# Low parts of the projections' weights: a negated copy by ScalarE and an adding DMA in place of a subtraction on VectorE

## The chip, the cores and the metric

The kernel runs on one core of a Trainium2 chip. The metric is the device time of one execution in microseconds, here the median of 3 runs: 1387.85 us (1387.84 to 1392.62). The profile is of one further execution, which took 1385.42 us; its span, from the first to the last instruction, is 1383.6 us. All times below are of that execution and count from the span's start.

The core has five engines with a program of their own: TensorE (matmuls, PE in the rows; PEld is its weight load), VectorE (DVE), ScalarE (ACT), GpSimd (POOL) and SyncE (SP), which issues most DMAs. DMAs run on 16 shared engines, whoever issues them. Each engine works its instructions off in order and waits on semaphores for others.

## The reference

One decoder block over a sequence of 1024 tokens of width 1024, in float32:

```python
ada = silu(c) @ w_ada + b_ada; sh1, sc1, gt1, sh2, sc2, gt2 = split(ada, 6)
h = rmsnorm(x, norm1_g) * (1 + sc1) + sh1
q, k, v, glu, gates = split(h @ w_in)
a = diff_attention(q, k, v, lam, rel_bias)          # 4 heads, two softmaxes each, causal
a = (rmsnorm(a, attn_sub_g) * (1 - lam_init)) @ w_o_attn
u = causal_depthwise_conv(u_lin * sigmoid(u_gate))  # 31 taps
cv = silu(layernorm(u)) @ w_o_conv + b_o_conv
y = sigmoid(g_attn) * a + sigmoid(g_conv) * cv
x = x + gt1 * (y @ w_out)
h2 = rmsnorm(x, norm2_g) * (1 + sc2) + sh2
fg, fu = split(h2 @ w_ffn_in)
x = x + gt2 * ((silu(fg) * fu) @ w_ffn_out)
return rmsnorm(x, final_g)
```

## The kernel before

Activations lie transposed, channels on the 128 partitions and tokens along the free axis, so a tile is 128 x 1024 and a matmul covers 128 x 512. To keep float32 accuracy with matmuls on a shorter format (fp32r), each operand is split into a high part, the value rounded to fp32r, and a low part, the value minus the high part. A product is then three matmuls, in this order (`mm3`, L203): high weights by high activations, high weights by low activations or the other way round, and one with the low weights. In the projections TensorE issues the one with the low weights third.

The class `Weights` (L171) makes the two parts of a slab of weights of 128 x 1024, in three steps. `load` (L176) fetches the raw weights by a DMA of SyncE (tile `wr_...`). `high` (L185) rounds them on ScalarE (`wh_...`). `low` (L189) subtracts on VectorE (`wl_...`). The pool has two buffers for each of the three tiles, so a part for one slab can be begun when the slab before last is no longer used: for the high and low parts, when its last matmul has ended.

Two planners call these steps ahead of use. In the attention stretch `project` (L679) works through 15 projections in 16 steps of three matmuls each, interleaved by the table `PLAN` with the work of the four heads; in step 2 of a projection it loads the raw weights of the next, in step 5 it makes the high part and in step 9 the low part (`WL`, L60). The first projection has no one before it: its three steps are called at once (L819). Behind the attention, `run` (L1025) goes through a list of jobs: gates of the attention (`ga`), its output projection (`oa`), gates of the convolution (`gc`), its output projection (`oc`), 48 matmuls each, and the common output projection (`wo`), 16 jobs of 24 matmuls. At a job's start it loads the next job's weights and makes their high part; the low part is made behind the first half of the job, in `wo` at its start. Weights of `oa` and `oc` come as two pieces of 512 columns, so their source has three dimensions.

The order of instructions on an engine is set by a scheduler that looks at what is ready, except where `in_order` keeps the order in which the code was written: TensorE in the attention stretch, TensorE and VectorE in the jobs up to `oc`. ScalarE's and GpSimd's orders are the scheduler's up to the FFN. In the convolution's norm (`ConvNorm`, L908), which lies between the jobs of `gc`, ScalarE computes squares, logarithms and exponentials. In `wo`, ScalarE squares each finished piece of x1 for the next norm (`sq`), and GpSimd issues the DMA that stores it (`x1_d`, L1136).

Of the kernel before, what the change touches and what calls it, by code (L numbers as in the profile page):

```python
# [10 lines left out]
F32 = mybir.dt.float32  # L11
F32R = mybir.dt.float32r
AF = mybir.ActivationFunctionType
ALU = mybir.AluOpType
# [85 lines left out]
def tile_hybrid_block(ctx: ExitStack, tc: tile.TileContext, xT, vecs, cvec, lamv, relb, bsel, bmask, jrev,  # L100
# [27 lines left out]
    V, A, T, G = Engine(nc.vector), Engine(nc.scalar), Engine(nc.tensor), nc.gpsimd  # L128
# [42 lines left out]
    class Weights:  # L171
# [15 lines left out]
            split_hi(self.hi[:, :self.n], self.raw[:, :self.n])  # L187

        def low(self):  # L189
            self.lo = wp.tile([P, D], F32R, tag="wlo", name=f"wl_{self.name}")  # L190
            V.tensor_tensor(out=self.lo[:, :self.n], in0=self.raw[:, :self.n], in1=self.hi.bitcast(F32)[:, :self.n],
                            op=ALU.subtract)

        def all(self):
            self.load()
# [698 lines left out]
    with tc.tile_pool(name="ps2", bufs=6, space=bass.MemoryType.PSUM) as ps2, ExitStack() as fxs:  # L894
# [71 lines left out]
        def ga(m, w, low):  # L966
            y.append(xslot(f"y{m}"))
            for hf in range(2):
                ps = (bankG if m == NGA else bank)("ga")
                gemm_half(ps, w, hacts, hf)  # L970
                A.activation(y[m][:, hf_sl(hf)], ps, AF.Sigmoid)
                advance(convs, CG[hf])
                if hf == 0:
                    low()
                    if m == NGA:
                        split_a(range(AS, H))

        def oa(m0, w, low):
            for i, m in enumerate((m0, m0 + 1)):
                for hf in range(2):  # L980
                    ps = bank("oa")
                    gemm_half(ps, [t[:, i * HB:(i + 1) * HB] for t in w], aacts, hf)
                    V.tensor_tensor(out=y[m][:, hf_sl(hf)], in0=ps, in1=y[m][:, hf_sl(hf)], op=ALU.mult)
                    advance(convs, CO[i])
                    if i == 0 and hf == 1:
                        low()
# [164 lines left out]
        class Pair:  # L1151
# [4 lines left out]
            n = HB  # L1156
# [111 lines left out]
        class Group(Pair):  # L1268

            n = GP * P  # L1270
# [269 lines left out]
        n = len(grp)  # L1540
# [132 lines left out]
```

## Time and profile before

| | |
|---|---|
| median of the runs | 1387.85 us |
| profiled execution, its span | 1385.42 us, 1383.6 us |
| TensorE busy | 1333.2 us (96%) |
| VectorE busy | 1067.0 us (77%) |
| ScalarE busy | 636.8 us (46%) |
| GpSimd busy | 104.1 us (8%) |
| attention stretch | about 100 to 363 us |
| `ga` and `oa` | 363 to 483 us |
| `gc` | 483 to 573 us |
| `oc` | 573 to 618 us |
| `wo` | 618 to 709 us |
| FFN and end | from 709 us |

A share of busy time is a mean over stretches with different limits; what a change in one stretch is worth is read in that stretch, from the wait that ends last there. A busy TensorE is not TensorE at its peak, since the ends of matmuls are modelled and overlap: in the stretches above one of 512 columns is begun each 0.23 us, while its row says 0.39.

### The profile page before, as it was taken

How to read it: one execution, taken by the hardware profiler on the slowest of the kernel's cores; microseconds unless marked ns; L12 is line 12 of the kernel's file. 1: busy time of each engine (PE TensorE's matmuls, PEld its weight loads, DVE VectorE, ACT ScalarE, POOL GpSimd, SP SyncE). 2: the span in 40 equal slices, each digit the busy share in tenths (PEclk: the TensorE clock that was granted, in tenths of full speed). 3: DMA queues.
4: the chain of work that ended last, by engine and by line, in shares of the span. 5: the costliest groups of instructions: out<-in, count | busy, mean ns of one | idle time of the engine just before them, and what ended most of it. 6: DMA issues, size and time to landing. Idle time of an engine off the chain costs nothing.

```text
span 1383.6 us, 16481 instructions
## 1 busy us (share of the span) xinstructions
PE 1333.2 (96%) x6070; PEld 1091.0 (79%) x6070; DVE 1067.0 (77%) x1698; ACT 636.8 (46%) x1079; POOL 104.1 (8%) x181
## 2 busy tenths in 40 slices
PE   7999999999999999999997999999999997999996
PEld 5678887877788887788775888888888886888886
DVE  6847698899989897787788677777777765777765
ACT  5546666666511114632575444444444441222355
POOL 0000000000000000000000011111100031212004
PEclk9999999999999999999999999999999999999998
DMA  8511010101112112329621255554444499578203
GB/s 304 192 32 31 32 46 16 47 16 31 46 46 61 46 61 92 137 92 343 234 77 77 76 183 183 182 166 167 157 165 147 150 315 398 203 250 304 74 31 122
DMA packets 58899, 184.43 MB, mean 133 GB/s; under 512 B 6425, under 2 KB 11457, under 8 KB 58818
## 3 DMA queue, kind: packets, MB, share of 16 engines
q1 hardware_dynamic: 38242, 110.49, 24.2%
q0 software_dynamic: 20000, 72.36, 14.7%
q8 instruction: 48, 0.79, 0.2%
q10 hardware_dynamic: 576, 0.52, 0.1%
q14 instruction: 33, 0.27, 0.1%
HBM read 139.83 MB, written 43.52 MB: 133 GB/s over the span
## 4 chain that ended last, share of the span: by engine, by line
PE 68%; issue 11%; DVE 9%; ACT 6%; DMA 5%; POOL 1%; SPq 0%; DVEq 0%; ACTq 0%; POOLq 0%
PE fx L113 19%; PE fz L113 9%; PE proj L113 8%; PE ga L113 5%; PE fy L113 5%; PE gc L113 4%; PE oa L113 3%; PE oc L125 3%; DMA ada<-in_w_ada 3%; PE wo L125 3%; PE sc L113 2%; PE vacc L125 2%; PE av L113 2%; DMA gb<-gs_d 1%; DMA xs<-in_xT 1%
## 5 line engine op out<-in xcount | busy, mean ns | idle before, releaser
L113 ACT ACTIVATE wbp<-tt 128x512 fp32r<-128x512 f32 (+1 forms) x75 | 43.9, 586 | 157.5 <-DVE tt L113 144.2
L113 DVE SCALAR_TENSOR_TENSOR cacc<-u,vec,cacc 128x1022 f32<-128x1022 f32 (+28 forms) x87 | 110.2, 1267 | 2.2
L113 PE MATMUL proj<-hhi,wh_in 128*128 128x512 f32 x239 | 98.3, 411 | 1.7 <-DVE kl L125 1.7
L113 PE MATMUL proj<-hhi,wl_in 128*128 128x512 f32 x240 | 94.0, 392 | 0.0
L113 PE MATMUL proj<-hlo,wh_in 128*128 128x512 f32 x240 | 93.7, 390 | 0.0
L113 ACT ACTIVATE wb<-tt 128x512 fp32r<-128x512 f32 (+1 forms) x59 | 35.4, 602 | 94.6 <-DVE tt L113 87.8
L113 PE MATMUL fx<-A,wb 128*128 128x512 f32 x299 | 70.9, 391 | 2.8 <-DVE g L113 2.8
L113 PE MATMUL fx<-gb,wbp 128*128 128x512 f32 x282 | 68.6, 389 | 0.1
L113 PE MATMUL fx<-S,wbp 128*128 128x512 f32 x276 | 67.1, 391 | 1.4 <-DVE S L113 1.3
L113 PEld LDWEIGHTS fx<-A,wb 128*128 128x128 f32 x299 | 56.0, 188 | 15.3 <-issue 3.7
L113 PE MATMUL fz<-S,wbp 128*128 128x512 f32 x276 | 66.5, 390 | 1.5 <-ACT S L113 1.3
L113 PE MATMUL fz<-S,wb 128*128 128x512 f32 x252 | 61.0, 390 | 1.6 <-DVE S L113 1.6
L113 PEld LDWEIGHTS fx<-S,wbp 128*128 128x128 f32 x276 | 51.6, 188 | 13.5 <-DVE S L113 2.5
L113 PE MATMUL fx<-S,wb 128*128 128x512 f32 x252 | 60.8, 390 | 1.4 <-DVE S L113 1.3
L113 PEld LDWEIGHTS fx<-gb,wbp 128*128 128x128 f32 x282 | 52.8, 188 | 11.5 <-DMA gb<-gs_d 0.5
L113 PEld LDWEIGHTS fz<-S,wbp 128*128 128x128 f32 x276 | 51.7, 188 | 12.9 <-ACT S L113 1.7
L113 DVE SCALAR_TENSOR_TENSOR x1r<-fx,cols,x1r 128x512 f32<-128x512 f32 x48 | 36.0, 751 | 30.6 <-PE fx L113 20.8
L125 ACT ACTIVATE e<-sc,mn 128x512 f32<-128x512 f32 (+7 forms) x64 | 47.2, 740 | 26.8 <-DVE mn L125 25.8
L113 PEld LDWEIGHTS fz<-S,wb 128*128 128x128 f32 x252 | 47.1, 188 | 12.1 <-DVE S L113 2.4
L113 PEld LDWEIGHTS fx<-S,wb 128*128 128x128 f32 x252 | 47.2, 188 | 11.9 <-DVE S L113 1.6
L113 DVE TENSOR_TENSOR wbp<-tt,wbp 128x512 fp32r<-128x512 f32 (+1 forms) x75 | 47.1, 629 | 11.7 <-ACT wbp L113 11.6
L113 PEld LDWEIGHTS proj<-hhi,wh_in 128*128 128x128 f32 x239 | 45.0, 188 | 11.1 <-issue 3.6
(350 smaller groups left out, 3601.9 us busy)
## 6 DMA issues: line engine op xcount, KB each, us to landing
gb<-gs_d POOLq DMA_DIRECT2D x59, 512.0 KB, 10.3
gs_d<-gstw POOLq DMA_DIRECT2D x36, 512.0 KB, 3.5
ada<-in_w_ada SPq DMA_DIRECT2D x32, 512.0 KB, 4.1
gs_d<-gst POOLq DMA_DIRECT2D x27, 512.0 KB, 4.3
rawu<-in_w_fi SPq DMA_DIRECT2D x22, 512.0 KB, 3.5
rawg<-in_w_fi SPq DMA_DIRECT2D x22, 512.0 KB, 4.4
adac<-in_w_ada SPq DMA_DIRECT2D x16, 512.0 KB, 4.8
wr_wo<-in_w_out SPq DMA_DIRECT2D x16, 512.0 KB, 5.1
```

The lines of the kernel that those rows point to most:

```text
L113: self.last = f(*args, **kw)
L125: self.last = self.chain(f, *args, **kw) if self.chain else f(*args, **kw)
```

## The change

`low` no longer subtracts. ScalarE writes the negated high part into the tile of the low part, and a DMA issued by GpSimd adds the raw weights from DRAM onto it (weights minus high part). The raw tile in SBUF is now read by `high` alone.

```diff
         def low(self):
+
             self.lo = wp.tile([P, D], F32R, tag="wlo", name=f"wl_{self.name}")
-            V.tensor_tensor(out=self.lo[:, :self.n], in0=self.raw[:, :self.n], in1=self.hi.bitcast(F32)[:, :self.n],
-                            op=ALU.subtract)
+            A.activation(self.lo[:, :self.n], self.hi[:, :self.n].bitcast(F32), AF.Copy, scale=-1.0)
+            if len(self.src.shape) == 3:
+                k = self.src.shape[0]
+                G.dma_start(self.lo[:, :self.n].rearrange("p (a n) -> p a n", a=k),
+                            self.src.rearrange("a p n -> p a n"), accum_op=ALU.add)
+            else:
+                G.dma_start(self.lo[:, :self.n], self.src, accum_op=ALU.add)
```

All 54 slabs of `Weights` go this way: 15 projections, 7 `ga`, 4 `oa`, 8 `gc`, 4 `oc` and 16 `wo`. The weights of the value projection, the first q and k and the FFN are split elsewhere and stay as they are.

ScalarE ahead of the first projection (`wh_in8` stands some 20 rows earlier; `vf` are values evacuated from PSUM, `vh0` the high part of head 0's values, `wh_in12` the second projection's weights), before:

```order
L125 ACTIVATE vf1_524<-vacc_577 128x128
L125 ACTIVATE vf2_525<-vacc_577 128x128
L125 ACTIVATE vf3_526<-vacc_577 128x128
L125 ACTIVATE vh0_794<-vf0_523 128x512
L125 ACTIVATE wh_in12_817<-wr_in12_806 128x1024
L125 ACTIVATE u0_798<-proj_799 128x512
```

and after:

```order
L125 ACTIVATE vf1_524<-vacc_577 128x128
L125 ACTIVATE vf2_525<-vacc_577 128x128
L125 ACTIVATE vf3_526<-vacc_577 128x128
L125 ACTIVATE wl_in8_791<-wh_in8_789 128x1024
L125 ACTIVATE vh0_795<-vf0_523 128x512
L125 ACTIVATE wh_in12_818<-wr_in12_807 128x1024
L125 ACTIVATE wl_in12_853<-wh_in12_818 128x1024
L125 ACTIVATE u0_799<-proj_800 128x512
```

The negation of the first projection's weights (`wl_in8`) stands behind the last of the values' evacuations; before, VectorE made that low part as soon as `wh_in8` was written.

ScalarE in the last jobs of `gc`, beside the convolution's norm (`rstd` are its logarithms and exponentials, `sgc` the gates), before:

```order
L125 ACTIVATE wh_gc7_4372<-wr_gc7_4370 128x1024
L125 ACT_TABLE_LOAD
L125 ACTIVATE sgc5_4275<-gc_4344 128x512
L125 ACT_TABLE_LOAD
L125 ACTIVATE rstd_4380<-var_4375,small_78 128x512
L125 ACTIVATE rstd_4382<-var_4376,small_78 128x512
L125 ACT_TABLE_LOAD
L125 ACTIVATE rstd_4380<-rstd_4380 128x512
L125 ACTIVATE rstd_4382<-rstd_4382 128x512
L125 ACT_TABLE_LOAD
```

and after:

```order
L125 ACTIVATE wh_gc7_4405<-wr_gc7_4403 128x1024
L125 ACT_TABLE_LOAD
L125 ACTIVATE sgc5_4307<-gc_4377 128x512
L125 ACT_TABLE_LOAD
L125 ACTIVATE rstd_4413<-var_4408,small_78 128x512
L125 ACTIVATE rstd_4415<-var_4409,small_78 128x512
L125 ACT_TABLE_LOAD
L125 ACTIVATE rstd_4413<-rstd_4413 128x512
L125 ACTIVATE rstd_4415<-rstd_4415 128x512
L125 ACTIVATE wl_gc7_4445<-wh_gc7_4405 128x1024
L125 ACT_TABLE_LOAD
```

The negation for `gc7` stands behind both exponentials.

ScalarE in the first jobs of `wo` before:

```order
L125 ACTIVATE wh_wo2_4917<-wr_wo2_4915 128x1024
L125 ACTIVATE sq_4909<-x1_0_4878 128x512
L125 ACTIVATE wh_wo3_4955<-wr_wo3_4953 128x1024
L125 ACTIVATE sq_4950<-x1_1_4919 128x512
L125 ACTIVATE wh_wo4_4993<-wr_wo4_4991 128x1024
L125 ACTIVATE sq_4988<-x1_2_4957 128x512
```

and after:

```order
L125 ACTIVATE wh_wo1_4903<-wr_wo1_4901 128x1024
L125 ACTIVATE wl_wo1_4919<-wh_wo1_4903 128x1024
L125 ACTIVATE yh7_4865<-sgc7_4487 128x512
L125 ACTIVATE wh_wo2_4957<-wr_wo2_4955 128x1024
L125 ACTIVATE sq_4949<-x1_0_4917 128x512
L125 ACTIVATE wl_wo2_4961<-wh_wo2_4957 128x1024
L125 ACTIVATE wh_wo3_4996<-wr_wo3_4994 128x1024
L125 ACTIVATE sq_4991<-x1_1_4959 128x512
L125 ACTIVATE wl_wo3_5000<-wh_wo3_4996 128x1024
```

The negation of a slab stands behind the square of the job that just ended. GpSimd's queue there after the change, where before only the stores `x1_d` stood:

```order
L198 DMA wl_wo1_4919<-in_w_out 128x1024
L1142 DMA x1_d_3208<-x1_0_4917 128x512
L198 DMA wl_wo2_4961<-in_w_out 128x1024
L1142 DMA x1_d_3208<-x1_1_4959 128x512
L198 DMA wl_wo3_5000<-in_w_out 128x1024
```

Adding DMAs and stores of x1 take turns.

## Rows read from the trace of the kernel before

**Rows 1.** Stretches: length, busy PE, PEld, DVE, ACT, POOL, clock, DMA share, GB/s.

```profile
100.00:363.00 263.00, 254.64 (x1312) 211.13 (x1312) 224.31 (x465) 176.63 (x328) 5.68 (x6) 1.00 0.10 31
...
483.00:573.00 90.00, 90.00 (x391) 73.09 (x391) 75.00 (x83) 38.20 (x48) 0.00 (x0) 1.00 0.29 98
...
618.00:709.00 91.00, 89.61 (x390) 72.79 (x390) 70.44 (x102) 41.98 (x59) 8.29 (x15) 1.00 0.69 246
```

**Rows 2.** TensorE's waits: total us, times, longest.

```profile
PE wo L125 <- DVE wl_wo L125: 1.2, 2, 0.8
```

**Rows 3.** Parts of the projections' weights: ns min/median/max, first and last start.

```profile
L125 DVE TENSOR_TENSOR wl_in<-wr_in,wh_in x15: 1215/1222/1226, 96.2 to 332.0; 128x1024 fp32r<-128x1024 f32 x15
L125 ACT ACTIVATE wh_in<-wr_in x15: 1042/1061/1166, 95.1 to 318.8; 128x1024 fp32r<-128x1024 f32 x15
```

**Rows 4.** DMA issues: queue, count, KB each, median us to landing.

```profile
gs_d<-gstw POOLq DMA_DIRECT2D x36, 512.0 KB, 3.5
...
wr_in<-in_w_in SPq DMA_DIRECT2D x15, 512.0 KB, 3.4
...
jr<-in_jrev SPq DMA_DIRECT2D x1, 64.0 KB, 1.8
```

**Rows 5.** Landing of GpSimd's 59 loads of 512 KB (tile `gb`).

```profile
DMA to landing us min/median/max: 3.5/10.3/19.8
```

**Rows 6.** DMA issues between 618 and 709 us.

```profile
wr_wo<-in_w_out SPq DMA_DIRECT2D x13, 512.0 KB, 5.2
```

**Rows 7.** ScalarE in order of time: start us, us, instruction.

```profile
102.52 0.75 ACT L125 ACTIVATE vh<-vf 128x512 fp32r<-128x512 f32 x1
```

**Rows 8.** TensorE, first matmul with a low part, at seven slabs.

```profile
100.67 0.40 PE L113 MATMUL proj<-hhi,wl_in 128*128 128x512 f32 x1
...
181.05 0.39 PE L113 MATMUL proj<-hhi,wl_in 128*128 128x512 f32 x1
...
527.02 0.39 PE L113 MATMUL gc<-hhi,wl_gc 128*128 128x512 f32 x1
...
563.19 0.39 PE L113 MATMUL gc<-hhi,wl_gc 128*128 128x512 f32 x1
...
624.16 0.39 PE L125 MATMUL wo<-yh,wl_wo 128*128 128x512 f32 x1
...
635.04 0.39 PE L125 MATMUL wo<-yh,wl_wo 128*128 128x512 f32 x1
...
703.57 0.39 PE L125 MATMUL wo<-yh,wl_wo 128*128 128x512 f32 x1
```

**Rows 9.** Two short stretches behind a wait, columns as in rows 1.

```profile
754.00:756.00 2.00, 1.29 (x6) 1.10 (x7) 1.90 (x4) 1.16 (x2) 0.00 (x0) 1.00 0.00 0
1153.40:1157.00 3.60, 3.52 (x9) 2.85 (x10) 1.95 (x4) 0.00 (x0) 0.54 (x1) 0.57 1.06 410
```

**Rows 10.** The waits ahead of them on TensorE (in brackets).

```profile
754.71 0.47 PE L113 MATMUL fx<-A,wb 128*128 128x512 f32 x1 [2.84 <-DVE g L113]
...
1153.48 0.76 PE L113 MATMUL fx<-gb,wb 128*128 128x512 f32 x1 [8.16 <-issue]
```

**Rows 11.** ScalarE where the negations will stand, in order of time.

```profile
172.99 0.60 ACT L125 ACTIVATE u<-proj 128x512 f32<-128x512 f32 x1
...
516.63 0.57 ACT L125 ACTIVATE sgc<-gc 128x512 f32<-128x512 f32 x1
...
557.15 1.15 ACT L125 ACTIVATE rstd<-rstd 128x512 f32<-128x512 f32 x2
...
618.34 1.05 ACT L125 ACTIVATE wh_wo<-wr_wo 128x1024 fp32r<-128x1024 f32 x1
...
629.17 1.06 ACT L125 ACTIVATE wh_wo<-wr_wo 128x1024 fp32r<-128x1024 f32 x1 [3.84 <-PE wo L125]
630.14 0.64 ACT L125 ACTIVATE sq<-x 128x512 f32<-128x512 f32 x1
...
640.05 1.06 ACT L125 ACTIVATE wh_wo<-wr_wo 128x1024 fp32r<-128x1024 f32 x1 [3.84 <-PE wo L125]
```

## The prediction

> **What bounds the kernel now.** I read the busy time by stretches first, since the change touches only the stretches from 100 to 709 us. There the reader sees TensorE busy for 254.64 of 263 us in the attention stretch, 90.00 of 90 in the stretch of the convolution's gates, and 89.61 of 91 in the output projection, at a granted clock of 1.00 [rows 1]. VectorE has 224.31 of 263 us in the first of them and ScalarE 176.63. So TensorE sets the time: 8.4 us (263 - 254.64) plus 1.4 us (91 - 89.61) is nearly all the idle time that a lighter VectorE could give back here. The list of waits names who is late: TensorE waits for a subtraction that makes a low part for only 1.2 us, in the output projection [rows 2]. Then I read, for each kind of projection, when the high part is ready and when TensorE first takes the low part, because the change replaces one short instruction between the two by a longer chain.
>
> **What it removes.** 54 subtractions of 1.222 us on VectorE [rows 3], 66 us of work. Beside a full TensorE this is worth at most the idle time above, 10 us; much of that hangs on other work of VectorE and on ScalarE, so I take 3 us, with 0 and 10 as ends.
>
> **What it adds.** Each low part now takes: a ScalarE pass over 128x1024 (the same shape as the high part, 1.061 us [rows 3]), the issue on GpSimd, and the landing of an adding DMA. No row shows such a DMA. From below: a plain store of the same 512 KB from GpSimd lands in 3.5 us [rows 4]. From above: GpSimd's loads of 512 KB, which run many at once, have a median of 10.3 us and a maximum of 19.8 [rows 5]. The adding DMA has to fetch the tile's old content as well as the weights. What another 512 KB costs, I estimate from a 64 KB load (1.8 us) and a 512 KB one (3.4 us): 1.6 us for 448 KB, so 1.8 us for 512 [rows 4]. That gives 3.5 + 1.8 = 5.3 us where the DMA engines are quiet, and I take it, as it is nearest to the store row. In the output projection the load of the weights alone takes 5.2 us at a median [rows 6], so there I take 7.0 us.
>
> The Trainium skill (Collectives: The Full Stack, "The bandwidth ceiling: the fold count and why AG ≠ RS ≠ AR") says that a reducing DMA is slower not for its addition but for its two source reads, which about halve the rate. No run here shows it yet; by the page an adding DMA at the store's 3.5 us would be the less likely end, and the estimate of 5.3 us would hardly move.
>
> The subtraction had its own place in VectorE's order. The negation stands in ScalarE's order behind what was ready there, and the DMA behind it. I go through the places.
>
> **First projection.** The negation stands behind the evacuations of the value projection, where the copy for head 0 starts at 102.52 us [rows 7]. It ends at 102.52 + 1.06 = 103.58, and the data lands 5.3 us later, at 108.9. TensorE takes this low part at 100.67 now [rows 8]: 8.2 us late. TensorE's order is fixed, so nothing fills the gap. A wait of 8.16 us later in this trace was followed by matmuls at a granted clock of 0.57, 9 of them in 3.52 us [rows 9, 10]; at full rate (90.00 us for 391, 0.23 each [rows 1]) 9 take 2.1. So 1.5 us come on top, 9.7 in all.
>
> The Trainium skill (TensorE: Matmul & The Clock Gate, "What's actually happening") says that an array left idle falls back from 2.4 to 1.2 GHz, whichever engine it waited for; the trace agrees, with 0.57 after the 8.16 us.
>
> **Other projections of the attention stretch, and the gates.** The tightest one has its negation behind a copy that starts at 172.99 and takes 0.60; it ends at 174.65, and TensorE takes the low part at 181.05: room for 6.4 us of landing [rows 8, 11]. A job of the gates: the sigmoid starts at 516.63, takes 0.57, the negation ends at 518.26, the low part is taken at 527.02: room for 8.8 us [rows 8, 11]. With 5.3 us both are hidden, by the matmuls of the projection before. On GpSimd's queue the adding DMAs of the attention stretch stand behind memsets of the key tiles, which wait for scores; I price this at nothing, since the negation behind them comes later than the scores they wait for. Without that cover a DMA would start some us late.
>
> **One gate beside the convolution's norm.** Its negation now stands behind two exponentials that end at 557.15 + 1.15 = 558.30. It ends at 559.4, and with 5.3 us it lands at 564.7, against 563.19 now: 1.5 us late [rows 8, 11]. An earlier negation also pushes that chain by up to 1.06 us. I take 2.
>
> **Output projection.** This is the main term. A job is only 24 matmuls, 5.44 us, and both buffers are in use, so low part i+2 can't be begun before job i ends. Now: a high part starts at 629.17, the next but one at 640.05, 10.88 us for two jobs [rows 11]. After: the square behind the high part ends at 630.14 + 0.64 = 630.78, the negation at 631.84, and 7.0 us of landing give 638.84, 9.67 us after 629.17. From the first use of a low part (635.04) to the next but one high part (640.05) are 5.01 us [rows 8, 11]. Two jobs take 9.67 + 5.01 = 14.68. Along the chain of odd jobs: the first negation follows the high part of 618.34 at once, so it ends at 618.34 + 1.05 + 1.06 = 620.45 and lands at 627.45 (taken at 624.16 now); seven periods later the last low part is taken at 627.45 + 7 x 14.68 = 730.2, against 703.57 now [rows 8, 11]. That is 26.6 us. GpSimd's stores of x1 stand between the adding DMAs, but each waits for an addition that comes before the negation, so they cost nothing. The loads of raw weights no longer wait for VectorE's subtraction, and TensorE gains nothing by it: it waits for the landing.
>
> **Sum.** 9.7 + 2 + 26.6 - 3 = 35.3 us. The profiled execution took 1385.42 us (its span is 1383.6): 1420.7. The median of the runs is 2.4 us above it, 1387.85, so I forecast 1423 us.
>
> **The likeliest case and its own range, 65%.** With 4.3 us quiet and 6.0 in the output projection: first projection 8.7, gate 1, output 18.6 (626.45 + 7 x 13.68 - 703.57), relief 5: +23, 1411. With 6.4 and 8.5: 10.8, 3, 38.6, relief 1: +51, 1439.
>
> **Rivals.**
> The landing is long, 10.3 us everywhere (GpSimd's loads come in crowds [rows 5]; here they come one at a time, which speaks against it). First projection 13.2 + 1.5; the tightest other projection 3.9 (10.3 - 6.4); of the jobs of gates and attention output, some 22, each half of 10.3 - 8.8, 16; the gate beside the norm 6; the output projection 630.75 + 7 x 17.98 - 703.57 = 53; less 3: +91, 1479. 13%.
>
> The clock falls with the waits of the output projection. A wait of 2.84 us left the clock at 1.00, one of 8.16 did not [rows 9, 10], and I expect waits of some 4 us in every second job or 2 in each. If each of 14 waits costs the 1.5 us above, 21 us come on top: 1444. 9%. The Trainium skill's rule on the clock gate, named above, would have it so if such waits count as an idle array.
>
> The adding DMA moves its data in small pieces and lands only after some 20 us. Then the first projection is 23 us late, the tightest other one 13.6 (the 15 together perhaps 100, an estimate at half of that), 22 jobs lose 5.6 each (123), and the output projection 640.45 + 7 x 27.68 - 703.57 = 131: near 1740. Nothing in the profile speaks for it. 4%.
>
> Not slower: the adding DMA lands like the store, in 3.5 us. The output projection then has a period of 11.2 us for two jobs, and its first low part lands at 623.95, before it is wanted: no loss. The gate is in time (562.9). The first projection is still 6.4 us late (107.1 against 100.67), which decides the sign: with all 10 us of idle time given back, 1387.85 + 6.4 - 10 = 1384. It turns on landing under about 3.8 us and on VectorE being behind nearly all idle time, of which the waits show little. 9%.
>
> 0.5% is 7 us, about what can be told from no change: faster means under 1381, slower over 1395. Only the last rival lies within it, and it gives 2% to faster and 7% to the same; the rest, 91%, is slower. The range for 8 in 10 runs from 1399 to 1480: it leaves out the last rival, the 20 us and part of the 10.3 us.
>
> **What would show it.** In the profile after, the landing of the adding DMAs: near 5 us up to 600 us, near 7 behind. TensorE waits some 8 us for the first low part at 100 us, with a lower clock just after, and not at all at the gates. The output projection runs over some 117 us for 91, with the chain of waits going through the negation and the DMA. If the landings are under 4 us, or the output projection keeps 91 us, the forecast is wrong; if the gates' jobs grow beyond 10.88 us, the landing is far longer than I take it.

## The result, and the profile after

The changed kernel takes 1450.95 us (median of 4 runs, 1450.63 to 1453.08), the kernel before 1388.37 us on the same chip. The ratio is 1.0446, 95% interval [1.0427, 1.0465]: 63 us slower. The forecast was 1423 us with a range of 1399 to 1480. Direction and places were right; the loss is nearly twice the one worked out. The profiled execution took 1450.72 us, its span is 1448.4.

Busy time by stretches of the changed kernel comes first, as in [rows 1] (length, PE, PEld, DVE, ACT, POOL, granted clock, DMA share, GB/s):

```profile
100.00:363.00 263.00, 245.81 (x1253) 203.66 (x1252) 194.59 (x425) 180.72 (x328) 19.78 (x22) 0.97 0.29 61
483.00:573.00 90.00, 90.00 (x391) 73.12 (x390) 70.93 (x75) 34.93 (x46) 6.05 (x7) 1.00 0.55 128
618.00:709.00 91.00, 71.39 (x277) 56.45 (x276) 42.78 (x69) 30.77 (x37) 12.93 (x17) 0.89 0.86 257
```

VectorE has less to do in every stretch, in part because less of the work falls into these us, and TensorE, which sets the time, has less done in two of them: 277 matmuls in the last 91 us where [rows 1] has 390. The gates' stretch is as full as before. The DMA engines went from 69% to 86% busy between 618 and 709 us, at nearly the same rate (246 GB/s before).

The list of TensorE's waits (total us, times, longest) names who is late now, where [rows 2] had 1.2 us for a subtraction:

```profile
PE wo L125 <- DMA wl_wo<-in_w_out: 31.0, 11, 5.4
PE proj L113 <- DMA wl_in<-in_w_in: 8.7, 1, 8.7
...
PE oc L125 <- DMA wl_oc<-in_w_oc: 1.9, 2, 1.3
...
PE gc L113 <- DMA wl_gc<-in_w_in: 1.6, 1, 1.6
...
PE ga L113 <- DMA wl_ga<-in_w_in: 0.9, 1, 0.9
```

These are 44 us of the 63. The first one in the order of time is the first projection. On ScalarE, GpSimd and TensorE there (start us, us, instruction, idle time before it and its releaser in brackets):

```profile
102.68 1.20 ACT L125 ACTIVATE wl_in<-wh_in 128x1024 fp32r<-128x1024 f32 x1
...
104.19 1.03 POOL L198 DMA_DIRECT2D wl_in<-in_w_in  x1 [100.63 <-ACT wl_in L125]
...
109.85 0.79 PE L113 MATMUL proj<-hhi,wl_in 128*128 128x512 f32 x1 [8.71 <-DMA wl_in<-in_w_in]
110.44 0.63 PE L113 MATMUL proj<-hhi,wh_in 128*128 128x512 f32 x1
110.87 0.63 PE L113 MATMUL proj<-hlo,wh_in 128*128 128x512 f32 x1
```

The negation ends at 103.88, the DMA is issued 0.3 us later and lands 5.6 us after that. The first use was at 100.67 [rows 8]. Behind the wait the matmuls start 0.43 us apart (110.44 to 110.87), where 391 in 90 us are 0.23 [rows 1]: the lower of the two clocks. The granted clock and the same behind a wait in the output projection, by the windows:

```profile
102.00:117.00 15.00, 7.15 (x24) 5.74 (x25) 2.04 (x4) 4.51 (x11) 1.89 (x2) 0.66 0.51 105
645.00:653.00 8.00, 3.66 (x9) 2.94 (x10) 2.07 (x6) 0.88 (x1) 1.00 (x2) 0.57 1.04 296
```

How the landings came out, by tile (min/median/max us), in the attention stretch and in the output projection; [rows 4] has 3.5 us for a plain store of the same 512 KB:

```profile
L198 POOL DMA_DIRECT2D wl_in<-in_w_in x15: 851/860/1061, 104.2 to 338.5; - x15
...
DMA to landing us min/median/max: 5.3/5.6/7.4
```

```profile
L125 PE MATMUL wo<-yh,wl_wo x128: 387/389/796, 638.2 to 771.7; 128*128 128x512 f32 x128
...
DMA to landing us min/median/max: 5.9/7.3/10.2
```

From the first to the last matmul with a low part the output projection takes 133.5 us (771.7 - 638.2), where it was 89.6 (618.7 to 708.3). One turn of its chain, on ScalarE, GpSimd and TensorE:

```profile
638.09 1.04 ACT L125 ACTIVATE wh_wo<-wr_wo 128x1024 fp32r<-128x1024 f32 x1
639.16 1.06 ACT L125 ACTIVATE wl_wo<-wh_wo 128x1024 fp32r<-128x1024 f32 x1
...
640.52 0.86 POOL L198 DMA_DIRECT2D wl_wo<-in_w_out  x1 [9.44 <-ACT wl_wo L125]
...
649.34 0.79 PE L125 MATMUL wo<-yh,wl_wo 128*128 128x512 f32 x1 [5.41 <-DMA wl_wo<-in_w_out]
650.78 0.63 PE L125 MATMUL wo<-yh,wl_wo 128*128 128x512 f32 x1
652.06 0.63 PE L125 MATMUL wo<-yh,wl_wo 128*128 128x512 f32 x1
653.08 0.39 PE L125 MATMUL wo<-yh,wl_wo 128*128 128x512 f32 x1
...
656.01 1.06 ACT L125 ACTIVATE wh_wo<-wr_wo 128x1024 fp32r<-128x1024 f32 x1 [10.13 <-PE wo L125]
```

The reader is to see a circle: high part at 638.09, negation to 640.22, issue at 640.52, use at 649.34, and only when that job is over the next but one high part, at 656.01. One turn is 17.92 us here, where [rows 11] show 10.88 (629.17 to 640.05); over the seven turns from the use at 649.34 to the last one at 765.20 the mean is 16.55. From the use to the next but one high part are 6.67 us where they were 5.01, since the matmuls behind the wait are at the lower clock: those with the low part, every third one, start 1.44, 1.28 and 1.02 us apart, where at full rate three matmuls take 0.69 (3 x 0.23).

### The profile page after: what moved, and what is told of

Same layout as the page of the kernel before. It is cut to its first block, busy times and chain, and to the rows that moved or that the text cites. A ratio compares the mean times of both kernels' runs of the same rounds, so it can differ in the third digit from the quotient of the medians.

```text
span 1448.4 us, 16619 instructions
## 1 busy us (share of the span) xinstructions
PE 1351.2 (93%) x6070; PEld 1100.3 (76%) x6070; DVE 1010.0 (70%) x1644; ACT 688.4 (48%) x1134; POOL 153.5 (11%) x235
## 4 chain that ended last, share of the span: by engine, by line
PE 56%; issue 23%; DVE 7%; DMA 6%; ACT 5%; POOL 3%; SPq 0%; POOLq 0%; DVEq 0%; ACTq 0%
PE fx L113 16%; PE fz L113 8%; PE proj L113 8%; PE gc L113 5%; PE ga L113 5%; PE fy L113 4%; DMA gb<-gs_d 3%; PE oa L113 3%; PE sc L113 2%; PE vacc L125 2%; PE av L113 2%; PE wps L113 1%; ACT kd L125 1%; POOL wl_wo L198 1%; DVE x L113 1%
## 5 line engine op out<-in xcount | busy, mean ns | idle before, releaser
L113 ACT ACTIVATE wbp<-tt 128x512 fp32r<-128x512 f32 (+1 forms) x75 | 43.9, 586 | 156.8 <-DVE tt L113 156.8
L125 PE MATMUL wo<-yh,wl_wo 128*128 128x512 f32 x128 | 55.8, 436 | 31.1 <-DMA wl_wo<-in_w_out 31.0
L113 PEld LDWEIGHTS proj<-hhi,wl_in 128*128 128x128 f32 x240 | 45.7, 190 | 19.3 <-DMA wl_in<-in_w_in 9.1
L125 PEld LDWEIGHTS wo<-yh,wl_wo 128*128 128x128 f32 x128 | 26.6, 208 | 42.2 <-DMA wl_wo<-in_w_out 36.6
```

Source lines behind the costliest of these rows:

```text
L113: self.last = f(*args, **kw)
L125: self.last = self.chain(f, *args, **kw) if self.chain else f(*args, **kw)
```

## The experiments

E1, E2, E3, E8 and E9 use the adding DMA for some slabs and VectorE's subtraction for the others. Their edit has one form, with another condition each (`...` stands for the branch for sources of three dimensions, as in the change):

```diff
+            if CONDITION:
                 A.activation(self.lo[:, :self.n], self.hi[:, :self.n].bitcast(F32), AF.Copy, scale=-1.0)
                 ...
                 G.dma_start(self.lo[:, :self.n], self.src, accum_op=ALU.add)
+            else:
+                V.tensor_tensor(out=self.lo[:, :self.n], in0=self.raw[:, :self.n],
+                                in1=self.hi.bitcast(F32)[:, :self.n], op=ALU.subtract)
```

**E1 and E2: where the loss sits.**

```diff
+            if self.name.startswith("wo"):       # E1: the output projection alone
+            if not self.name.startswith("wo"):   # E2: all the others
```

> Only the 16 slabs of the output projection take their low part by the adding DMA; the other 38 by VectorE's subtraction. Theory (the time is lost where the negation, the DMA's issue and its landing are later than the next job wants them): all of the output projection's loss comes back by itself, 31 us of waits and about 10 us of lower clock behind them: before + 42, 1430 us. Rival (each adding DMA costs the same, through traffic or ScalarE's time, wherever it stands): 16 of 54 of the 63 us, before + 19, 1407 us.

> The complement: adding DMAs for 38 slabs, the subtraction for the 16 of the output projection. Theory: first projection 8.7 us of wait and about 1.8 us of lower clock, small waits at a gate's projection, at the last gate beside the norm and in the convolution's output, some 5 us, and 3 to 4 us that the attention stretch lost: before + 20, 1408 us. Rival (the same cost per DMA): 38 of 54 of 63 us, before + 44, 1432 us.

E1: 1431.98 us, ratio 1.0315 [1.0289, 1.0340], 44 us over the kernel before (1387.91, measured beside it). E2: 1405.67, ratio 1.0123 [1.0105, 1.0141], 18 over. The two losses add up to 62 of the 63. So 70% of the loss comes from 16 of 54 DMAs; a price per DMA is refuted. TensorE's waits in E1 and in E2:

```profile
PE wo L125 <- DMA wl_wo<-in_w_out: 33.2, 9, 7.1
```

```profile
PE proj L113 <- DMA wl_in<-in_w_in: 8.8, 1, 8.8
...
PE gc L113 <- DMA wl_gc<-in_w_in: 1.8, 1, 1.8
```

**E3: the first projection.**

```diff
+            if self.name != "in8":
```

> The changed kernel, with one slab alone, that of the first projection, back on VectorE's subtraction. Theory: the wait of 8.7 us and the 1.8 us of lower clock behind it go, and nothing else is late in its place: 1451 - 10.5 = 1440 us. Rival: what stands behind it (ScalarE's and VectorE's work for the first scores) was late by nearly as much, and the wait only moves: 1451 - 3 = 1448 us or more.

1440.06 us (1437.68 to 1448.52), ratio 1.0382 [1.0347, 1.0417]: by the medians 10.9 us less than the changed kernel, 10.5 were expected. One slab of 54 costs a sixth of the whole loss, its wait and the lower clock behind it.

**E4: the addition itself.** The low part is the raw weights here; the subtraction is left out, also in the branch for sources of three dimensions.

```diff
-                G.dma_start(self.lo[:, :self.n], self.src, accum_op=ALU.add)
+                G.dma_start(self.lo[:, :self.n], self.src)
```

> The changed kernel, with the same negation, the same queue and the same DMAs, but these copy the weights over the tile and add nothing (so the low part is the weights themselves: the subtraction is left out). Theory (an adding DMA lands later than a plain one because it reads the tile's old content too): landing 3.5 us for 5.6 where it is quiet and 5.2 for 7.3 in the output projection; there every second job waits 2.1 us less, 16 us, some 7 us of lower clock go with them, and 2 us in the first projection: 1451 - 25 = 1426 us. Rival (the landing is what a 512 KB DMA of GpSimd takes here anyway, adding is free): landings of 5.6 and 7.3 stay, 1451 us.

1425.05 us, ratio 1.0263 [1.0248, 1.0278]: 26 us less. The median landing is 4.0 us in the attention stretch (5.6 with the addition) and 5.5 in the output projection (7.3). TensorE's waits:

```profile
PE wo L125 <- DMA wl_wo<-in_w_out: 17.1, 12, 2.4
...
PE proj L113 <- DMA wl_in<-in_w_in: 7.1, 1, 7.1
```

So the addition costs 1.6 us a slab, 1.8 where the DMA engines are loaded, for the estimate of 1.8. The landing counts from the start of the issue, and 0.33 us of the difference are the issue itself: GpSimd takes 0.86 us for it with the addition and 0.53 without. Some seven tenths of the landing are there without it, and so are 37 us of the loss. What GpSimd's queue takes of the 16 DMA engines between 618 and 709 us (packets, MB, share), in the changed kernel and in E4:

```profile
q0 software_dynamic: 2128, 7.08, 35.4%
```

```profile
q0 software_dynamic: 2544, 8.59, 25.6%
```

That is 5.0% of the engines for a MB with the addition and 3.0% without, 1.7 times as much, the stores of `x1` included. The Trainium skill (Collectives: The Full Stack, "The bandwidth ceiling: the fold count and why AG ≠ RS ≠ AR") says of a reduce that its two source reads about halve the rate; the engines' time here comes near to that, the landing (1.4 times as long) does not.

**E5: ScalarE's place without the DMA.**

```diff
             A.activation(self.lo[:, :self.n], self.hi[:, :self.n].bitcast(F32), AF.Copy, scale=-1.0)
-            G.dma_start(self.lo[:, :self.n], self.src, accum_op=ALU.add)
+            V.tensor_tensor(out=self.lo[:, :self.n], in0=self.raw[:, :self.n],
+                            in1=self.lo.bitcast(F32)[:, :self.n], op=ALU.add)
```

> ScalarE writes the negation as in the changed kernel, and VectorE adds the raw weights on it in SBUF: the same result, no DMA. It keeps ScalarE's place and load and takes away the issue and the landing. Theory (the landing is the cost): the first low part comes 103.6 + 1.2 us, 4 us late, and nothing else is late: before + 5, 1393 us. Rival (the negation's place in ScalarE's order is the cost): the output projection stays long, over 1420 us.

1410.97 us, ratio 1.0168 [1.0153, 1.0183]. For the output projection the theory holds: 92.4 us from its first to its last low part, for 133.5 with the DMA. So the negation's place in ScalarE's order, with VectorE's addition behind it, costs 3 us there, and the issue and the landing cost the rest. But the total missed: 23 us over the kernel before, where 5 were expected. The attention stretch took most of them. Matmuls with `wl_in` (ns; first and last start), in E1, whose attention stretch is as before, and in E5:

```profile
L113 PE MATMUL proj<-hhi,wl_in x240: 387/389/398, 102.0 to 364.5; 128*128 128x512 f32 x120
```

```profile
L113 PE MATMUL proj<-hhi,wl_in x240: 387/389/628, 105.6 to 382.4; 128*128 128x512 f32 x120
...
  ACT wl_in L125: 5.1, 6
```

From the first to the last are 262.5 us in E1, 276.8 in E5. VectorE's additions there wait for the negations (5.1 us, 6 times), and what stands behind them on VectorE waits with them. That this makes up the 14 us was not shown. In the changed kernel they are 267.0 (109.9 to 376.9): for the attention stretch this way is worse than the DMA.

**E6: room in the job.** The 16 matmuls with the high part first, the 8 with the low part last.

```diff
-            gemm_half(ps, w, yacts, hf)
+            for k, (ah, al) in enumerate(yacts):
+                for t in (ah, al):
+                    T.matmul(ps, w[0][:, k * P:(k + 1) * P], t[:, hs], start=k == 0 and t is ah, stop=False)
+            for k, (ah, al) in enumerate(yacts):
+                T.matmul(ps, w[1][:, k * P:(k + 1) * P], ah[:, hs], start=False, stop=k == KD - 1)
```

> The changed kernel, but a job of the output projection does its 16 matmuls with the high part first and the 8 with the low part last. The low part is wanted 3.6 us later in its job and the buffer is free at the same time, so from a job's end to the use of the next but one low part are 14.5 - 5.4 = 9.1 us, for the negation (1.05), the issue (0.3) and the landing (7.3): 8.7. Theory: waits nearly all gone, the clock stays up, 36 to 40 us come back: 1413 us. Rival (the output projection is slow because the DMA engines are full there, 86% busy): it only waits elsewhere, over 1435 us.

1432.95 us, ratio 1.0334 [1.0313, 1.0356]: 18 us come back, not 38. The waits fall to 21.5 us only: the landing of 7.3 us that was counted on is the median of the whole projection, and where the traffic is densest it is longer, in the changed kernel too. TensorE's waits in E6; the DMA issues between 618 and 709 us (count, KB, median landing) in E6, then in the changed kernel:

```profile
PE wo L125 <- DMA wl_wo<-in_w_out: 21.5, 8, 6.7
```

```profile
wr_wo<-in_w_out SPq DMA_DIRECT2D x11, 512.0 KB, 8.7
wl_wo<-in_w_out POOLq DMA_DIRECT2D x10, 512.0 KB, 9.2
```

```profile
wr_wo<-in_w_out SPq DMA_DIRECT2D x10, 512.0 KB, 8.5
wl_wo<-in_w_out POOLq DMA_DIRECT2D x9, 512.0 KB, 8.8
```

The raw weights' loads land in 8.7 and 8.5 us where [rows 6] have 5.2, and in E6 they delay the high part on ScalarE itself:

```profile
691.79 1.06 ACT L125 ACTIVATE wh_wo<-wr_wo 128x1024 fp32r<-128x1024 f32 x1 [5.84 <-DMA wr_wo<-in_w_out]
```

Both theories are half right: the circle was a limit, since 18 us come back with the order alone, and the traffic looks like the next one.

**E10: less traffic.** E6, which also leaves out 14 of the 16 raw loads of the output projection (`...` stands for the lines that put the last two raw tiles into `kept`).

```diff
+            if self.name[:2] == "wo" and int(self.name[2:]) >= 2:
+                self.raw = kept[int(self.name[2:]) % 2]
+                return
 ...
```

> The kernel with the high part's matmuls first (e6_high_first), which also leaves out 14 of the 16 loads of raw weights in the output projection (the high parts are made from the first two; the adding DMAs stay). Theory (e6_high_first kept 21.5 us of waits because the DMA engines are full there: the raw loads land in 8.7 us for 5.2, the adding DMAs in 8.4): the adding DMAs land in 6 to 7 us, the waits fall under 5 us: 1433 - 18 = 1415 us. Rival (the adding DMA is slow by itself, or its place in ScalarE's order is): 1428 us or more.

1425.87 us (1420.23 to 1428.04), ratio 1.0262 [1.0242, 1.0281]: 7 us less than E6, 18 were expected. The waits are 15.4 us, the median landing is 7.8 us for 8.4. So the raw loads are a part of it. Another part is new, on GpSimd's queue:

```profile
678.69 0.57 POOL L1153 DMA_DIRECT2D x_d<-x  x1 [4.18 <-DVE x L125]
679.25 0.91 POOL L205 DMA_DIRECT2D wl_wo<-in_w_out  x1
```

The negation for this DMA ended at 675.47 (674.41 + 1.06), and its DMA (679.25) stands behind a store of `x1` that waits for VectorE until 678.69: 3.8 us from negation to issue instead of 0.3. In the changed kernel each adding DMA of the output projection is issued 0.3 us after its negation, so the stores cost nothing there, as predicted; here VectorE's additions come later than the negations, and the stores cost. The landings between 618 and 709 us moved little (9.2 in E6):

```profile
wl_wo<-in_w_out POOLq DMA_DIRECT2D x11, 512.0 KB, 8.6
```

With the raw loads gone, 22 other loads of 512 KB are left there (`ada`, `x` and two of the FFN's weights). Between 700 and 725 us, where none of them is issued, the four adding DMAs land in 5.8 us at a median. So the traffic that counts may be these loads; no run left them out.

**E11: smaller pieces.**

```diff
-                G.dma_start(self.lo[:, :self.n], self.src, accum_op=ALU.add)
+                for c in range(0, self.n, HB):
+                    G.dma_start(self.lo[:, c:c + HB], self.src[:, c:c + HB], accum_op=ALU.add)
```

> The changed kernel, with each adding DMA of one slab split into two of 256 KB, for the first four and the last four blocks of the slab; TensorE needs the second 12 matmuls (2.8 us) after the first. Theory (the landing grows with the bytes): the first half lands about 1.5 us sooner, in the first projection 7.3 us of wait for 8.7, in the output projection 1.5 to 2 us less in every second job, with less time at the lower clock: 1451 - 20 = 1431 us. Rival (the two halves share the DMA engines, the first lands as late as the whole, and GpSimd issues twice): 1451 to 1460 us.

1440.76 us, ratio 1.0373 [1.0355, 1.0392]: 10 us less, half of what was expected. (`oa` and `oc`, whose sources have three dimensions, keep one DMA each slab.) The first projection waits 7.2 us for 8.7, as expected; the output projection 22.2 for 31.0. Its clock stays low (0.89 from 618 to 709 us).

**E7: the clock in the output projection.**

```diff
+            if i % 2:
+                for k in range(12):
+                    T.matmul(ps, w[0][:, k % KD * P:(k % KD + 1) * P], yacts[k % KD][0][:, hs], start=True, stop=True)
             gemm_half(ps, w, yacts, hf)
```

> The changed kernel, with 12 more matmuls (2.8 us at full rate, their result is overwritten) ahead of every second job of the output projection, where TensorE waits up to 5.4 us for the low part. Theory (the long jobs behind the waits are the lower clock, and an array that is kept at work keeps it): the fillers go into the waits, the granted clock stays at 1.00, some 8 us come back: 1443 us. Rival (the jobs are long for another reason): the same or longer, 1451 to 1460 us.

1448.83 us, ratio 1.0431 [1.0412, 1.0450], not to be told from 1.0446 [1.0427, 1.0465]. The fillers did hold the clock in part. Windows of E7 (columns as above):

```profile
660.00:680.00 20.00, 16.33 (x60) 12.91 (x59) 5.88 (x10) 5.20 (x6) 2.85 (x4) 0.83 0.91 289
...
720.00:740.00 20.00, 19.53 (x85) 15.48 (x84) 3.64 (x5) 10.02 (x12) 4.27 (x6) 1.00 0.79 178
```

Three of the 16 jobs are long now, for six. From the first to the last low part of a job, summed over the jobs, they take 85.0 us for 88.3, and 76.6 before. That is 3 of 12 us given back; the median is 2.1 us lower, within the intervals. The expected 8 us didn't come: the fillers are matmuls too, and together with the waits that are left (14.8 us, and 96 fillers of 0.23 us make 22) they take 37 us for 31. That the long jobs run at the lower clock is shown by the windows; what that clock costs in the end is put at these 12 us, not measured by itself.

**E8 and E9: hidden slabs alone.** The adding DMA for the 31 slabs whose low part was in time; E9 puts the negation on GpSimd.

```diff
+            if self.name[:2] not in ("wo", "oc") and self.name not in ("in8", "ga2", "gc7"):
-                A.activation(self.lo[:, :self.n], self.hi[:, :self.n].bitcast(F32), AF.Copy, scale=-1.0)   # E9
+                G.tensor_scalar(out=self.lo[:, :self.n], in0=self.hi[:, :self.n].bitcast(F32), scalar1=-1.0,
+                                scalar2=None, op0=ALU.mult)                                                # E9
```

> The adding DMA only for the 31 slabs whose low part was in time after the change: all of the attention stretch but the first and the last, the gates but the one beside the norm, the attention output; the subtraction for the other 23. Theory: no wait for a DMA; TensorE is full, so VectorE's relief gives little, and the attention stretch loses the 2 to 3 us that it lost beside its two known waits: before + 2, 1390 us. Rival (relief counts once nothing is late): before - 5, 1383 us.

> The same 31 hidden slabs as in the kernel before it (e8_hidden), but GpSimd writes the negation, so VectorE and ScalarE are both relieved of it. Theory (e8_hidden's 2.5 us are ScalarE's 31 negations, which push its exponentials and evacuations in the attention stretch): they go, and VectorE's relief is left: before - 1, 1387 us, at best 1385. Rival (VectorE's relief is worth nothing and GpSimd's pass is slow or disturbs VectorE): 1391 us or more.

E8: 1390.72 us, ratio 1.0029 [1.0015, 1.0043]; E9: 1392.04, ratio 1.0024 [1.0014, 1.0033]. Neither gains, and the two are alike. The matmuls with `wl_in` in E8 and in E9:

```profile
L113 PE MATMUL proj<-hhi,wl_in x240: 387/390/632, 101.9 to 367.7; 128*128 128x512 f32 x120
L125 ACT ACTIVATE wl_in<-wh_in x14: 1044/1048/1062, 105.5 to 327.8; 128x1024 fp32r<-128x1024 f32 x14
```

```profile
L113 PE MATMUL proj<-hhi,wl_in x240: 387/389/628, 101.6 to 367.4; 128*128 128x512 f32 x120
L193 POOL TENSOR_SCALAR wl_in<-wh_in x14: 2760/2778/3791, 105.3 to 326.3; 128x1024 fp32r<-128x1024 f32 x14
```

Both need 265.8 us from the first to the last, for 262.5 in E1: 3.3 us lost with nearly no wait for a low part. E9 takes the negations off ScalarE and loses as much, so ScalarE's load, which was the theory of E9, doesn't explain it. What both share is a VectorE whose list has lost its subtractions. Its order, and ScalarE's, is left to the scheduler there, and it came out another way. VectorE in E1 and in E8, at the same place:

```profile
184.18 1.22 DVE L125 TENSOR_TENSOR wl_in<-wr_in,wh_in 128x1024 fp32r<-128x1024 f32 x1
185.31 0.16 DVE L125 RECIPROCAL mn<-mn 128x2 f32<-128x2 f32 x1
185.56 0.69 DVE L125 TENSOR_REDUCE mn<-sc 128x1 f32<-128x512 f32 x1
...
187.72 1.14 DVE L125 SCALAR_TENSOR_TENSOR e<-e,mn 128x896 f32<-128x896 f32 x1
```

```profile
185.99 0.69 DVE L125 TENSOR_REDUCE mn<-sc 128x1 f32<-128x512 f32 x1 [1.88 <-PE sc L113]
186.59 0.15 DVE L125 RECIPROCAL mn<-mn 128x2 f32<-128x2 f32 x1
...
189.31 1.15 DVE L125 SCALAR_TENSOR_TENSOR e<-e,mn 128x896 f32<-128x896 f32 x1
```

In E1 the reciprocal comes before the reduction of the next scores. In E8 the subtraction is gone and the reciprocal stands behind that reduction, which waits 1.88 us for TensorE. The product of the softmax ends 1.6 us later, and TensorE's transposes start at 190.52 for 188.92. E5 tells more: it has no DMA there and an addition on VectorE in place of the subtraction, yet its reciprocal (192.90) also stands behind that reduction (192.29, a wait of 0.78 us for TensorE). Over the eight low-part matmuls of this place (181.05 to 188.97 before) E5 loses 2.0 us and E8 2.1. So this loss needs neither an adding DMA nor relief; what E5 and E8 share here is the order. The rest of the 3.3 us arises later and was not traced to one cause: around 310 us TensorE waits up to 1.5 us at a time for the keys' parts from ScalarE and VectorE (up to 1.0 in E1), and then works for a while at the lower clock (granted 0.82 from 310 to 316 us in E8, 0.52 in E9, 1.00 in E1).

**E12: the kernel before with E6's order.**

> The kernel before, with the output projection's high-part matmuls first and no adding DMA. Theory: it takes away the 1.2 us that TensorE waits for a subtraction there, and nothing else: 1388 - 1 = 1387 us. Rival: the loads of raw weights set the pace, and the order of the matmuls does nothing, 1388 us.

1388.14 us, ratio 0.9995 [0.9984, 1.0006]: no difference. No version here beats the kernel before.

## Why the prediction was right, and where it was not

Worked out from the two traces by how much later each slab's low part is first used than before (the stretch ahead of 100 us, which the change doesn't touch, varies by up to 1.3 us between executions: 102.0 in E1 for 100.7):

| term | predicted | in the trace |
|---|---|---|
| first projection, wait and clock | 9.7 | 11.0 |
| relief of VectorE | -3 | +2.7 in the attention stretch |
| other gates' projections | 0 | 1.2 |
| gate beside the norm | 2 | 1.8 |
| convolution's output | 0 | 2.8 |
| output projection | 26.6 | 43.9 |
| behind it | 0 | 1.5 |
| sum | 35.3 | 64.9 |

**Right.** The landing was worked out as 5.3 us quiet and 7.0 loaded, and the medians are 5.6 and 7.3 (8.8 between 618 and 709 us, below). The first projection was to wait 8.2 us and waits 8.7, and E3 shows that its 11 us are its own. The gates are hidden, but for 0.9 us at one of them. The rivals with a long landing, with small pieces and of no loss are refuted by these landings.

**The output projection: the term was mis-sized, 26.6 for 43.9 us.** The mechanism was right: two buffers, and a chain from the negation to the landing (E1, E5). Three sizes were not, and the period of 14.68 us came out at 16.55: 13.1 of the missing 17.3 us in the seven turns, 2.4 us ahead of the first of them and 1.8 in the last job. First, the landing was taken as 7.0 in each turn, but between 618 and 709 us the median is 8.8, the turn shown has 8.8 too, and between negation and issue lie 0.3 us that the sum left out. Second, the jobs behind a wait were taken at full rate. I had the clock as a rival with 9%, and it is part of what happened: 12 us more in the jobs' own matmuls, about half of that rival's 21. E7 gave back only 3 of them. The rows had a wait of 2.84 us that left the clock at 1.00 and one of 8.16 that did not [rows 9, 10], and I took the 4 us that I expected to lie on the safe side. They did not: the six long jobs stand behind waits of 5.41, 4.05, 3.40, 5.25, 2.88 and 1.90 us (granted clock 0.63 to 0.76 over each), while the jobs behind 3.06 and 2.08 us keep their length (1.00). So the length of the one wait ahead doesn't tell whether the clock falls. The Trainium skill (TensorE: Matmul & The Clock Gate, "What's actually happening") has it that the clock goes by how busy the array has been, so that an idle one falls to the lower level; the windows agree, with 0.57 behind the wait of 5.41 us for a DMA. Third, the adding DMAs load the DMA engines in the very stretch where they are fullest, so that the raw loads, whose 5.2 us the 7.0 was built on, take 8.5 there; E4 shows landings that move with the addition, and E10 has 5.8 us for 8.6 once the other loads are over.

**VectorE's relief: the step failed, in its sign.** The prediction bounded it by 0 and 10 us, with idle time of TensorE as the measure. E8 and E9 take 31 subtractions off VectorE and lose 3 to 4 us (0.29% and 0.24%). The bounds left out that an engine whose order a scheduler sets doesn't keep its order when an instruction is taken out of it or replaced; E5 and E8 lose some 2 us where the new order stands, and what the rest hangs on stays open.

**The convolution's output** was left at nothing. Its adding DMAs land in 7.0 us (median; 9.5 at most) and TensorE waits 1.9 us: the same chain with little room, which the list of places passed over.

## What to carry to other kernels

A DMA in place of an engine's short instruction is hidden only where the room between the last free buffer and the use exceeds issue and landing together: work that out for each place, by the slowest landing where the traffic is densest, not by a median. Where buffers close a circle, the landing counts once in every turn, and a clock that falls behind the wait lengthens the turn again. Relief of an engine that isn't the bound may be worth nothing, and less than nothing where the scheduler then orders it anew.

## What the runs showed of the hardware

GpSimd needs 0.86 us to issue an adding DMA of 512 KB, and 0.53 us without the addition. The addition makes such a DMA land 1.6 us later in quiet (5.6 for 4.0) and 1.8 later under load (7.3 for 5.5). The same negation of 128 x 1024 takes 1.05 us on ScalarE and 2.78 on GpSimd. Waits of TensorE of 5.41, 2.88 and 1.90 us were followed by the lower clock, waits of 3.06, 2.84 [rows 10] and 2.08 were not: the length of one wait alone doesn't tell.
